# Selected heads projected behind the first branch, selection one round a step, retention's values ahead of the second branch

## Chip, cores and metric

The kernel runs on one core of a Trainium2 chip. The metric is device time in microseconds, the median of the runs shown. PE is the matrix engine (PEld its weight loads), DVE the vector engine, ACT the scalar engine, POOL GpSimd, SP the queue that issues the loads.

## The reference, cut to what matters

The program is one block of a first architecture (S5 and gating branches, cross attention, a gated feed-forward) followed by two layers of a second one; sequence 512, width 1024, fp32. The change is in the mixing stage of the second architecture, which each of its two layers runs once:

```python
h = rmsnorm(x, attn_norm[l]);  z = h @ w_in[l]
(qA, kA, vA, fA, qB, kB, vB, qI, kI, wI, qC, kC, vC, gC, qD, kD, vD, gates) = split(z)
yA = forgetting_attention(qA, kA, vA, fA, forget_bias[l])            # 8 heads, causal
yB = dsa_attention(rope(qB), rope(kB), vB, rope(qI), rope(kI), wI)   # 8 heads, top 128 keys of a row
r  = retention(rope(qC), rope(kC) * 64**-0.5, vC)
yC = head_groupnorm(r, ret_norm[l]) * silu(gC)
yD = sliding_window_gqa(rope(qD), rope(kD), vD, attn_sinks[l])       # window 128
branch = einsum('bsnc,ncd->bsnd', stack([yA, yB, yC, yD]), w_branch[l])
merged = sum(sigmoid(gates) * branch, axis=branches)
x = x + merged @ w_out[l]
```

In `dsa_attention` each query keeps the `topk = min(256, 512 // 4) = 128` keys with the highest index score, a sum over four index heads; the others are masked out.

## The kernel before

**Projections.** Everything is kept transposed: features on the 128 partitions, the 512 tokens along the free dimension. fp32 values are split into two fp32r parts, and each product is three matmuls (`mm3`, L184). One projection of 128 features (`gemm_b`, L190) is 8 slices of the width times 3, thus 24 matmuls of 512 columns; a natural-layout projection of 512 features (`gemm_a`, L198, through `natural`, L1249) is 96 such matmuls into four PSUM banks at once. `weights` (L177) loads 512 KB into one of two `raw` buffers on SP's queue; ACT copies the upper part `hi` (L166) and DVE subtracts to get `lo` (L111), each in one of three buffers.

**Buffers.** 48 tiles of the tag `g`, 12 of `h`, 10 of `tmp`; PSUM banks are 4 `mm` for projections, 3 `sc` for scores and transposes, 1 `pv` for attention's output.

**Order of the work.** Attention, selection and retention are Python generators that stand in two lists. `pump(n)` (L140) takes one step of the list `bg2`, which holds the selection alone, and `n` steps of the list `bg`, oldest generator first; `drain` (L150) runs the named generators to their end. So a program order comes about in which a step of attention or selection stands behind a projection. The framework's scheduler then lays out each engine's queue at build time on a simulated timeline: instructions that are ready can be taken ahead of earlier ones that are not, as far as buffers allow.

**Stages of `mix2` (L1319).** The first rotated projections give the index heads and the selected heads' key; `select` (L1115) is started; a misc projection and the fox values (`natural`, L1338 on) follow. Then the fox loop projects key and query of four pairs of heads, builds a `fox_pair` (L1072) for each and appends it to `bg`, with `rate` 4. The selected heads' loop projects four pairs of rotated queries (at the first of them the selection is drained, since the masks are needed) and appends a `rope_pair` for each. `branch` 0 follows with a lead of 4 gates, then the window heads with `rate` 2, `branch` 1, retention's values, gates, keys and queries, `branch` 3, `branch` 2 and the output projection.

**A branch (L1255).** For each of 8 slices of the output it needs a gate (a projection, times the row norm, tanh; 24 matmuls) and a product of the branch's output with its weights (12 matmuls). `lead` gates come first, then the attention that feeds the branch is drained, then slices and remaining gates alternate. The first branch writes its gates in the merged tiles, later ones in `tmp`. Each gate and each slice pumps once.

**Attention (`attend`, L966).** A pair of heads takes 14 steps: per chunk of 128 queries the scores and their maximum (PE, DVE, L982), then exponentials (ACT), sums and normalization (DVE, L994 and L996), then transposes (PE, L1007) and copies (ACT, L1010); at the end all value matmuls (PE, L1021) and a split of the result.

**Selection (`select`).** Three scoring steps, one for each chunk of queries from the second on. Then 16 rounds, each of which finds the 8 largest scores of a row (MAX8, L1144) and strikes them out (MATCH_REPLACE8 with its value load, L1145) in the three chunks; a step holds two rounds (L1146). A last step turns what was struck out into a mask (L1150).

**Retention (`retain`, L1153).** 31 steps over four chunks; it reads the values `vc` from tiles of the tag `h`, which the fox values `va` use before.

Of the kernel before, what the change touches and what calls it, by code (L numbers as in the profile page):

```python
# [11 lines left out]
AF = mybir.ActivationFunctionType  # L12
# [5 lines left out]
P = 128  # L18
# [10 lines left out]
MAGIC = 12582912.0  # L29
LEAD = (4, 3, 3, 3)  # L30
NSLOT = 48
# [40 lines left out]
class Builder:  # L72
# [1042 lines left out]
    def select(self, si, hh, ll, msc):  # L1115
# [24 lines left out]
        for r in range(16):  # L1140
            for c in range(1, CHUNKS):
                sc = self.masks[c]
                m8 = self.t(ap, [P, 8], "m8", bufs=3)
                nc.vector.max(m8, sc)  # L1144
                nc.vector.match_replace(sc, m8, sc, -3.0e38)  # L1145
            if r % 2:  # L1146
                yield
        for c in range(1, CHUNKS):
# [105 lines left out]

    def branch(self, l, n, y, x, first, gens=(), lead=3):  # L1255


        nc = self.nc
        gs = []

        def gate(d):
            bk = self.bank("mm")
            self.gemm_b(bk, self.weights(self.I["w_gates"][l, n, d], KT * P), x)
            g = self.merged[d] if first else self.tmp()
            self.mul(g, bk, self.rb)
            self.act(g, g, AF.Tanh, scale=0.5)
            gs.append(g)
            self.pump(self.rate)

        for d in range(lead):  # L1270
            gate(d)
        self.drain(*gens)
        wb = None
        for d in range(KT):
            if d + lead < KT:
                gate(d + lead)
            if d % 2 == 0:
# [41 lines left out]
    def mix2(self, l):  # L1319
# [29 lines left out]
        ya, yb, yc, yd = {}, {}, {}, {}  # L1349
        ga, gb, gd = [], [], []  # L1350
        for j in range(4):
            bk = self.project(I["w_fox"][l, 4 + j], x)
            self.pump(self.rate)
            bq = self.project(I["w_fox"][l, j], x)
            ga.append(self.fox_pair(ya, j, bq, bk, va))
            self.bg.append(ga[-1])
            self.pump(self.rate)

        for j in range(4):
# [8 lines left out]
            self.pump(self.rate)  # L1368
        self.branch(l, 0, ya, x, True, ga, LEAD[0])
        self.rate = 2  # L1370
# [4 lines left out]
        for j in range(4):  # L1375
# [10 lines left out]
            self.pump(self.rate)  # L1386
        self.branch(l, 1, yb, x, False, gb, LEAD[1])

        vc = [self.g2() for _ in range(CHUNKS)]
        self.natural(I["w_vc"][l], x, vc, 512)  # L1390
        sg = [self.g() for _ in range(CHUNKS)]
        rn = self.g()
# [222 lines left out]
```

## Time and profile before

| | us |
|---|---|
| median of 3 runs | 3055.34 |
| lowest, highest | 3055.07, 3061.35 |
| profiled execution, its own time | 3054.14 |
| its span in the trace | 3052.3 |
| PE busy in the span | 2979.2 |
| DVE busy | 1993.9 |
| ACT busy | 1354.3 |

Times in the views are microseconds from the span's start. The mixing stage of the first layer lies at about 940 to 1600 us, that of the second at about 1980 to 2640 us. A wait is put down to what ended it. The busy time of a window counts overlapping instructions of an engine once; the busy time of a group adds their records, which overlap a little. The granted clock is TensorE's, as a share of full speed.

### The profile page before, as it was taken

The numbers are of one execution on the slowest core, as the hardware profiler recorded it, in microseconds if no ns is written. First come the engines' busy times: TensorE is split into PE (matmuls) and PEld (weight loads), VectorE is DVE, ScalarE is ACT, GpSimd is POOL, SyncE is SP. The second block draws the span as 40 slices with busy tenths as digits, with TensorE's granted clock in tenths as the row PEclk, the third lists the DMA queues.
The fourth block names the chain that finished last, engine by engine and source line by source line (L and its number), as shares of the span: only waits on it lengthen the run. The fifth ranks groups of instructions, "written<-read, shape, count | busy, mean of one in ns | idle before, by whom it ended". The sixth has DMA issues, their size and how long they took to land.

```text
span 3052.3 us, 38841 instructions
## 1 busy us (share of the span) xinstructions
PE 2979.2 (98%) x14882; PEld 2481.1 (81%) x14882; DVE 1993.9 (65%) x3850; ACT 1354.3 (44%) x2271; POOL 112.2 (4%) x148
## 2 busy tenths in 40 slices
PE   9999899999999998999999999999899999999998
PEld 7888888888888877887888888888687788888887
DVE  7887564545447796556667566569866466675575
ACT  5523443422226565546234333356665453343343
POOL 0000000011010000000000010000000000000010
PEclk9999999999999999999999999999999999999999
DMA  5233442333333221222133333342122222323332
GB/s 171 83 92 99 113 162 84 100 92 95 104 90 122 88 75 42 69 83 91 63 117 105 97 92 103 92 136 78 54 70 67 82 80 82 125 92 99 97 95 82
DMA packets 98362, 287.09 MB, mean 94 GB/s; under 512 B 12144, under 2 KB 20592, under 8 KB 98176
## 3 DMA queue, kind: packets, MB, share of 16 engines
q1 hardware_dynamic: 95712, 283.04, 29.7%
q10 hardware_dynamic: 2464, 1.57, 0.3%
q8 instruction: 117, 1.92, 0.3%
q14 instruction: 69, 0.57, 0.1%
HBM read 274.64 MB, written 9.93 MB: 93 GB/s over the span
## 4 chain that ended last, share of the span: by engine, by line
PE 91%; DVE 5%; ACT 2%; DMA 1%; issue 1%; SPq 0%; DVEq 0%; ACTq 0%
PE psmm L186 27%; PE psmm L187 27%; PE psmm L188 27%; PE pspv L1021 2%; PE pssc L1007 1%; DVE g L111 1%; DVE lo L111 1%; PE pssc L1110 1%; PE pssc L1111 0%; DVE tmp L111 0%; DVE prob L982 0%; PE pspv L806 0%; DMA raw<-w_down 0%; PE pssc L774 0%; PE pssc L716 0%
## 5 line engine op out<-in xcount | busy, mean ns | idle before, releaser
L186 PE MATMUL psmm<-g,hi 128*128 128x512 f32 (+1 forms) x3456 | 1342.8, 391 | 14.7 <-DVE h L111 4.9
L188 PE MATMUL psmm<-g,lo 128*128 128x512 f32 (+1 forms) x3456 | 1344.4, 390 | 3.5 <-DVE lo L111 3.5
L187 PE MATMUL psmm<-g,hi 128*128 128x512 f32 (+1 forms) x3456 | 1343.3, 389 | 0.0
L166 ACT CAST hi<-raw 128x1024 fp32r<-128x1024 f32 (+3 forms) x507 | 508.7, 1004 | 1168.9 <-PE psmm L187 839.2
L186 PEld LDWEIGHTS psmm<-g,hi 128*128 128x128 f32 x3456 | 650.0, 188 | 151.6 <-DVE g L111 4.0
L188 PEld LDWEIGHTS psmm<-g,lo 128*128 128x128 f32 x3456 | 650.7, 188 | 138.1 <-DVE lo L111 5.9
L187 PEld LDWEIGHTS psmm<-g,hi 128*128 128x128 f32 x3456 | 650.9, 188 | 128.8 <-issue 0.8
L111 DVE TENSOR_TENSOR lo<-raw,hi 128x1024 fp32r<-128x1024 f32 (+3 forms) x507 | 608.7, 1201 | 209.7 <-ACT hi L166 208.6
L111 DVE TENSOR_TENSOR tmp<-psmm,g 128x512 f32<-128x512 f32 x236 | 161.6, 688 | 287.5 <-PE psmm L188 276.3
L1461 DVE SCALAR_TENSOR_TENSOR g<-psmm,g 128x512 f32<-128x512 f32 x88 | 60.8, 691 | 150.2 <-PE psmm L188 150.2
L186 PE MATMUL psmm<-hi,g 128*128 128x512 f32 (+1 forms) x384 | 143.7, 381 | 9.9 <-ACT g L123 7.1
L187 PE MATMUL psmm<-lo,g 128*128 128x512 f32 (+1 forms) x384 | 145.4, 379 | 0.0
L111 POOL TENSOR_TENSOR tmp<-tmp,tmp 128x512 f32<-128x512 f32 x66 | 89.0, 1349 | 1531.4 <-DVE tmp L1435 521.0
L188 PE MATMUL psmm<-hi,g 128*128 128x512 f32 (+1 forms) x384 | 142.9, 375 | 0.0
L1435 DVE SCALAR_TENSOR_TENSOR tmp<-tmp,vec,tmp 128x510 f32<-128x510 f32 (+1 forms) x176 | 132.8, 757 | 2.5 <-ACT tmp L123 1.2
L111 DVE TENSOR_TENSOR g<-tmp,g 64x512 fp32r<-64x512 f32 (+2 forms) x166 | 113.4, 684 | 17.9 <-ACT g L166 11.0
L123 ACT ACTIVATE prob<-prob,nmx 128x128 f32<-128x128 f32 (+2 forms) x192 | 102.6, 535 | 41.8 <-DVE nmx L982 37.6
L1010 ACT COPY probT<-pssc 128x128 f32<-128x128 f32 (+2 forms) x192 | 70.1, 400 | 74.1 <-PE pssc L1007 73.4
L939 ACT COPY tmp<-psmm 32x512 f32<-32x512 f32 x160 | 92.5, 578 | 2.4
L123 ACT ACTIVATE tmp<-tmp 128x512 f32<-128x512 f32 (+1 forms) x138 | 84.2, 613 | 20.9 <-DVE tmp L111 18.3
L1007 PE MATMUL pssc<-idn,prob 128*128 128x128 f32 x432 | 70.4, 283 | 23.3 <-DVE prob L996 22.3
L186 PEld LDWEIGHTS psmm<-hi,g 128*128 128x128 f32 x384 | 73.7, 192 | 22.3 <-ACT g L123 7.1
(275 smaller groups left out, 2688.2 us busy)
## 6 DMA issues: line engine op xcount, KB each, us to landing
raw<-w_up SPq DMA_DIRECT2D x110, 512.0 KB, 3.5
raw<-w_gates SPq DMA_DIRECT2D x64, 512.0 KB, 3.5
raw<-w_down SPq DMA_DIRECT2D x72, 384.0 KB, 3.1
raw<-w_rope SPq DMA_DIRECT2D x40, 512.0 KB, 3.6
raw<-w_branch SPq DMA_DIRECT2D x32, 512.0 KB, 3.5
raw<-w_out SPq DMA_DIRECT2D x24, 512.0 KB, 3.5
raw<-w_gate SPq DMA_DIRECT2D x22, 512.0 KB, 3.6
raw<-w_fox SPq DMA_DIRECT2D x16, 512.0 KB, 3.5
```

Source lines behind the costliest of these rows:

```text
L111: (eng or self.nc.vector).tensor_tensor(out, a, b, op)
L123: self.nc.scalar.activation(out, in_, func, **k)
L166: nc.scalar.copy(hi, src)
L186: mm(out, sh, mh, start=start, stop=False)
L187: mm(out, sh, ml, start=False, stop=False)
L188: mm(out, sl, mh, start=False, stop=stop)
L939: nc.scalar.copy(xs[k * 32:k * 32 + 32], bk[(k ^ 1) * 32:(k ^ 1) * 32 + 32])
L1007: nc.tensor.transpose(tr[:, j * P:(j + 1) * P], pt[i][:, j * P:(j + 1) * P], self.ident)
L1010: nc.scalar.copy(ptT, tr[:, :n * P])
L1021: nc.tensor.matmul(pv[i * 64:(i + 1) * 64, pc * P:(pc + 1) * P], value(i, b), tt[i][:, j * P:(j + 1) * P], start=j == 0, stop=j == len(bl) ...
L1435: nc.vector.scalar_tensor_tensor(o[:, sh:], u[:, :S - sh], w, o[:, sh:], ALU.mult, ALU.add)
L1461: self.nc.vector.scalar_tensor_tensor(self.x[d], ps, 0.5, self.x[d], ALU.mult, ALU.add)
```

## The change

Four edits in `mix2`, `branch` and `select`. The gate of a branch becomes a method, `gate`, and `branch` takes gates that are already there. In the fox loop one gate of the first branch is projected behind each pair, and behind the loop `branch` 0 is called with the four gates and a lead of 8, so its other four gates come before the drain of fox attention. The selected heads' loop stands behind that branch, still with `rate` 4, and still with the drain of the selection at its first projection. The selection yields after each round instead of each second one. Retention's values are projected before `branch` 1 instead of after it. The leads of the other branches are unchanged at 3.

```diff
--- before.py
+++ after.py
@@ -27,7 +27,7 @@
 NL = 2
 CHUNKS = 4
 MAGIC = 12582912.0
-LEAD = (4, 3, 3, 3)
+LEAD = {1: 3, 2: 3, 3: 3}
 NSLOT = 48
 NSLOT2 = 12
 NTMP = 10
@@ -1143,8 +1143,7 @@
                 m8 = self.t(ap, [P, 8], "m8", bufs=3)
                 nc.vector.max(m8, sc)
                 nc.vector.match_replace(sc, m8, sc, -3.0e38)
-            if r % 2:
-                yield
+            yield
         for c in range(1, CHUNKS):
             sc = self.masks[c]
             nc.vector.tensor_scalar(sc, sc, -1e37, NEG, ALU.is_gt, ALU.mult)
@@ -1252,28 +1251,28 @@
         for c in range(CHUNKS):
             self.act(out[c][:, :ncol], banks[c][:, :ncol], AF.Copy, scale=self.rc[:, c:c + 1])
 
-    def branch(self, l, n, y, x, first, gens=(), lead=3):
+    def gate(self, l, n, d, x, first):
+
+        bk = self.bank("mm")
+        self.gemm_b(bk, self.weights(self.I["w_gates"][l, n, d], KT * P), x)
+        g = self.merged[d] if first else self.tmp()
+        self.mul(g, bk, self.rb)
+        self.act(g, g, AF.Tanh, scale=0.5)
+        self.pump(self.rate)
+        return g
+
+    def branch(self, l, n, y, x, first, gens=(), lead=0, gs=()):
 
 
         nc = self.nc
-        gs = []
-
-        def gate(d):
-            bk = self.bank("mm")
-            self.gemm_b(bk, self.weights(self.I["w_gates"][l, n, d], KT * P), x)
-            g = self.merged[d] if first else self.tmp()
-            self.mul(g, bk, self.rb)
-            self.act(g, g, AF.Tanh, scale=0.5)
-            gs.append(g)
-            self.pump(self.rate)
-
-        for d in range(lead):
-            gate(d)
+        gs = list(gs)
+        while len(gs) < lead:
+            gs.append(self.gate(l, n, len(gs), x, first))
         self.drain(*gens)
         wb = None
         for d in range(KT):
-            if d + lead < KT:
-                gate(d + lead)
+            if len(gs) < KT:
+                gs.append(self.gate(l, n, len(gs), x, first))
             if d % 2 == 0:
                 wb = self.weights(self.I["w_branch"][l, n, d // 2], 1024)
             bb = self.bank("mm")
@@ -1347,7 +1346,7 @@
         self.natural(I["w_va"][l], x, va, 512)
         self.fox_rows(f)
         ya, yb, yc, yd = {}, {}, {}, {}
-        ga, gb, gd = [], [], []
+        ga, gb, gd, g0 = [], [], [], []
         for j in range(4):
             bk = self.project(I["w_fox"][l, 4 + j], x)
             self.pump(self.rate)
@@ -1355,6 +1354,8 @@
             ga.append(self.fox_pair(ya, j, bq, bk, va))
             self.bg.append(ga[-1])
             self.pump(self.rate)
+            g0.append(self.gate(l, 0, len(g0), x, True))
+        self.branch(l, 0, ya, x, True, ga, KT, g0)
 
         for j in range(4):
             o = proj(4 + j)
@@ -1366,7 +1367,6 @@
                                      lambda c: list(range(c + 1))))
             self.bg.append(gb[-1])
             self.pump(self.rate)
-        self.branch(l, 0, ya, x, True, ga, LEAD[0])
         self.rate = 2
 
         kd, kdl = self.stack_k(proj(1))
@@ -1384,10 +1384,10 @@
                 lambda j: self.vec(f"sink{l}")[:, 2 * j:2 * j + 2]))
             self.bg.append(gd[-1])
             self.pump(self.rate)
-        self.branch(l, 1, yb, x, False, gb, LEAD[1])
 
         vc = [self.g2() for _ in range(CHUNKS)]
         self.natural(I["w_vc"][l], x, vc, 512)
+        self.branch(l, 1, yb, x, False, gb, LEAD[1])
         sg = [self.g() for _ in range(CHUNKS)]
         rn = self.g()
         nc.sync.dma_start(rn, I["ret_norm"][l].partition_broadcast(P))
```

## Rows read from the trace of the kernel before

**Rows 1.** The page: busy time, share of the span and instructions of each engine.

```profile
PE 2979.2 (98%) x14882; PEld 2481.1 (81%) x14882; DVE 1993.9 (65%) x3850; ACT 1354.3 (44%) x2271; POOL 112.2 (4%) x148
```

**Rows 2.** Waits of PE, first layer (930:1560): total us, times, longest.

```profile
PE pssc L1007 <- DVE prob L996: 11.8, 5, 4.2
```

**Rows 3.** Waits of PE, second layer (1990:2680), same columns.

```profile
PE pssc L1007 <- DVE prob L996: 10.5, 5, 3.2
```

**Rows 4.** Windows: length, busy us of PE, PEld, DVE, ACT, POOL; clock; DMA.

```profile
1040.00:1060.00 20.00, 20.00 (x94) 16.65 (x93) 19.74 (x46) 16.01 (x29) 0.52 (x1) 1.00 0.24 79
...
1160.00:1180.00 20.00, 16.49 (x99) 13.97 (x100) 8.72 (x33) 9.38 (x27) 0.00 (x0) 0.76 0.00 1
...
1280.00:1300.00 20.00, 18.97 (x119) 15.30 (x115) 15.07 (x38) 14.24 (x33) 0.00 (x0) 1.00 0.09 27
1300.00:1320.00 20.00, 18.12 (x115) 14.77 (x116) 16.92 (x44) 11.77 (x30) 0.00 (x0) 1.00 0.24 80
...
1600.00:1620.00 20.00, 20.00 (x90) 16.55 (x89) 11.95 (x15) 8.67 (x12) 0.00 (x0) 1.00 0.54 181
```

**Rows 5.** Windows of whole stretches, same columns.

```profile
1032.00:1182.00 150.00, 135.84 (x704) 111.00 (x706) 133.99 (x343) 100.70 (x205) 2.08 (x4) 0.95 0.19 60
2075.00:2220.00 145.00, 131.82 (x693) 107.81 (x692) 131.08 (x334) 99.37 (x198) 2.08 (x4) 0.96 0.20 64
...
1147.00:1182.00 35.00, 26.13 (x154) 21.00 (x152) 20.56 (x65) 21.67 (x58) 0.00 (x0) 0.84 0.03 11
1183.00:1305.00 122.00, 120.38 (x716) 100.17 (x712) 73.29 (x172) 70.49 (x152) 0.00 (x0) 1.00 0.22 70
...
1100.00:1182.00 82.00, 68.25 (x381) 54.84 (x379) 66.39 (x187) 53.77 (x121) 0.52 (x1) 0.91 0.12 39
2140.00:2222.00 82.00, 68.70 (x408) 55.19 (x408) 68.64 (x195) 54.03 (x122) 0.52 (x1) 0.94 0.14 45
```

**Rows 6.** DVE's groups in 1032:1182: shapes xcount; busy us, mean ns; idle before.

```profile
L1145 DVE MATCH_REPLACE8 g<-m,g 128x384 f32<-128x384 f32 (+2 forms) x47 | 25.3, 543 | 0.1
L1144 DVE MAX8 m<-g 128x8 f32<-128x384 f32 (+2 forms) x47 | 24.4, 548 | 0.0
L111 DVE TENSOR_TENSOR lo<-raw,hi 128x1024 fp32r<-128x1024 f32 x17 | 20.6, 1211 | 0.0
L111 DVE TENSOR_TENSOR g<-tmp,g 64x512 fp32r<-64x512 f32 x24 | 16.4, 683 | 0.6
...
L111 DVE TENSOR_TENSOR tmp<-psmm,g 128x512 f32<-128x512 f32 x12 | 7.9, 678 | 0.0
...
L1145 DVE MATCH_VALUE_LOAD g<-m,g 128x8 f32 x47 | 3.7, 78 | 0.1
...
L111 DVE TENSOR_TENSOR tmp<-tmp,g 128x512 f32<-128x512 f32 x4 | 2.7, 678 | 0.0
L111 DVE TENSOR_TENSOR tmp<-tmp,tmp 128x512 f32<-128x512 f32 x4 | 2.7, 676 | 0.0
```

**Rows 7.** PE's groups in 1032:1182, same columns; one of three alike.

```profile
L186 PE MATMUL psmm<-g,hi 128*128 128x512 f32 x140 | 54.9, 399 | 3.6 <-ACT hi L166 1.8 <-DVE h L111 1.8
```

**Rows 8.** Timeline of DVE, end of the selection: start us, us, instruction.

```profile
1142.09 0.54 DVE L1150 TENSOR_SCALAR g<-g 128x256 f32<-128x256 f32 x2
...
1142.62 0.68 DVE L1145 MATCH_REPLACE8 g<-m,g 128x512 f32<-128x512 f32 x1
...
1143.81 0.41 DVE L1150 TENSOR_SCALAR g<-g 128x512 f32<-128x512 f32 x1
```

**Rows 9.** Timeline of PE: value matmuls of three fox pairs.

```profile
1145.18 2.40 PE L1021 MATMUL pspv<-probT,h 128*64 128x128 f32 x38
...
1164.76 3.53 PE L1021 MATMUL pspv<-probT,h 128*64 128x128 f32 x38
...
1181.63 3.62 PE L1021 MATMUL pspv<-probT,h 128*64 128x128 f32 x38
```

**Rows 10.** Timeline of SyncE's queue: loads around 1145 us.

```profile
1145.38 53.99 SPq L174 DMA_DIRECT2D raw<-w_rope  x4
```

## Prediction

> **What bounds the kernel now.** I read the page's busy table first: PE is busy 98% of the span (3052.3 us in the table), DVE 65% [rows 1]. So there is little to win outside PE's gaps, and the next question is where they lie. The waits of PE name one consumer in both layers of the second block: transposes of attention probabilities (L1007) that wait for DVE's normalization, 11.8 us in five waits in the first layer and 10.5 us in the second [rows 2, 3]. The windows then show the shape in time [rows 4]. At 1040 to 1060 us DVE has 19.74 of 20 us busy and PE is full. At 1160 to 1180 us DVE is down to 8.72 us, PE to 16.49, and the granted clock to 0.76 of full speed. Two regimes follow each other: one in which DVE is full, one in which a chain hops between PE, DVE and ACT and PE has nothing else.
>
> DVE's groups say what fills the first [rows 6]: 47 MAX8 and 47 MATCH_REPLACE8 of the selection with their value loads, 53.4 us by their records, the largest item by far. The selection's last replacement starts at 1142.62 us and its last mask at 1143.81 [rows 8]. From there forgetting attention's pairs run unhindered: their value matmuls come at 1145.18, 1164.76 and, for the fourth pair, 1181.63 us, so a pair takes some 17 to 20 us [rows 9]; two of four pairs were still to do. PE can't fill the time because SyncE's row shows four loads of projection weights spread over 54 us from 1145.38 [rows 10]: behind the branch weights the loads stand still until attention is through.
>
> **The change part by part.** No instruction is added or removed: the same 64 gate projections, 32 selection rounds, loads and evacuations, on the same engines. What changes is their order, so the sum is one of waits.
>
> *What the pumps do.* A pump runs one step of the selection and `rate` steps of attention. Before, the value projection pumps once and the fox loop 8 times: 3 scoring steps and 6 double steps, thus 12 of 16 rounds, with 28 of 56 attention steps. The first selected head then drains the other 4 rounds and the masks, ahead of the second half of attention. After, the fox loop pumps 12 times and the four other gates 4 times: 17 selection steps are 3 of scoring and 14 rounds (13 by the pump that writes attention's 56th step), the rest goes into the branch's own 8 pumps. So the selection is spread evenly instead of leading, and 3 rounds and the masks fall behind the first attention.
>
> *DVE up to the end of fox attention.* Between 1032 and 1182 us DVE has 133.99 us busy [rows 5]. Records overlap, so I scale each record total by 0.89 (133.99 over the 150 us that the groups of this stretch add up to, of which eight are shown). The selected heads' projections go behind: 12 tensor operations of 0.68 us in their rotation, 8 residues of 0.683 and 4 weight splits of 1.211 [rows 6], 18.5 us of records, 16.4 scaled. The 3 late rounds are 9 times (0.543 + 0.548 + 0.078) us, 10.5, and 0.95 for the masks [rows 8], 10.2 scaled. DVE needs then 107.4 us if these stay behind and 117.6 if the scheduler pulls the always ready rounds forward. It would end at 1139 or 1150 us; I take the middle, 1145, and some 3 us for the last hop: 1148.
>
> *PE up to there.* PE was busy 135.84 us in this stretch, at a mean clock of 0.95 [rows 5]. The moved projections are 96 of the 420 matmuls of 512 columns (three groups of 140 [rows 7]), at 90 in 20 us [rows 4] 21.3 us. That leaves 114.5 us, or 107 if the clock's 5% (7.5 us) came back whole: 1139 to 1147, say 1143. PE's and DVE's demand now meet. PE's idle time there falls from 14.2 us (150 less 135.84) to about 5 us, and the clock's share from 7.5 to about 3: 13.7 us in the first layer. In the second the same stretch is 145 us long with 131.82 busy at 0.96 [rows 5], 13.2 and 5.8 us against the same 5 and 3: 11.0 us. Together 24.7 us. The bounds are 40.7 us (all of both layers) and nothing below the rival's loss.
>
> Over 1100 to 1182 and 2140 to 2222 us PE sits idle 13.75 and 13.30 us of 82, while weight loads cover 54.84 and 55.19 us; in the dense stretch 1183 to 1305 they cover 100.17 of 122 [rows 5]. The Trainium skill (Perfetto Trace Analysis, "Identifying the Most-Contended Engine") says that matmul busy time flatters PE and that weight-load busy time is the better measure; by it I estimate 15.2 and 14.8 us lost, 3 us more than PE's own gaps, and a gain larger by that.
>
> *Selected heads and the second branch.* Their projections now come when masks are nearly done, so their attention can start once the first is rotated, about where it started before. What covers it grows: beside the window heads' five projections and the branch's gates, as now, three of its own four projections and the values of retention (96 matmuls, 21.3 us). But its steps run at 4 a pump for only 4 pumps, then at 2 for the window heads' 4, the values' 1 and the 3 leading gates: 32 of 56. The other 24 are drained in one go, where before none were. At 17 us per 14 steps that is 29 us, beside gates 3 to 7, 120 matmuls or 26.7 us, and attention's own matmuls. The branch lost 1.03 and 1.88 us at 1280 to 1320 [rows 4]; I let that grow by 2.5 us a layer, between a gain of 2.9 (cover complete) and a loss of 12 (no gate is pulled forward, at the loss of 1147 to 1182: 8.9 us idle of 35 and 16% of the clock, 5.6 us [rows 5]). Cost: 5 us.
>
> *Small things.* The four loads of retention's values move ahead of the branch's on SyncE, behind the window heads'; nothing on PE waits for them earlier than now. GpSimd's queue keeps its order. Their four output tiles take the buffers of the fox values, last read by the value matmuls that start at 1181.63 us [rows 9], before the window heads are even projected. The values take all four PSUM banks at once, behind a rotation instead of behind the branch; the latter wait moves to the gates of retention. The window heads end later, by 3 pumps, and so does retention, whose 31st step now falls on the last pump ahead of its branch; gate 3's 24 matmuls, 5.3 us, lie behind it. I cost these at nothing, between minus 2 and plus 4 us a layer if that one gate is too short.
>
> **Sum.** 24.7 less 5 is 19.7 us off the profiled execution's 3054.14 us (span 3052.3 and 1.8 around it): 3034.4. The median shown, 3055.34, lies 1.2 us above that execution, so 3035.
>
> **Rivals.**
> - *The cover was needed more than the selection hurt (slower).* Four projections leave the stretch in which PE starves, and the first three branch weights hold the three weight buffers as soon as the gates are through. 13 of 16 rounds still precede attention's last step. If the fourth pair runs alone once DVE is free, at 17 us, it ends near 1163; PE, ready at 1143, idles 20 us, and loses 7.5 to the clock as now: 27.5 against 21.7, 5.8 us a layer worse, with the drain 2 times 8.3: 3072. It decides from an end of attention after some 1155 (11.7 us idle). For it: two pairs do run alone now. Against: they do so because the selection was drained ahead of them, which the change undoes.
> - *Moved, not removed (no change).* The drain of 24 steps costs its 12 us a layer and eats the gain: 24.7 less 24, 3055. For it: before, such a stretch was where the clock fell. Against: gates were pulled ahead of the stalled first branch, and five are at hand.
> - *The order hardly changes.* The scheduler takes selection rounds whenever DVE is free, so their place in the program matters little: DVE ends at 1150, attention at 1153, PE idles 10 us and the clock costs 5: 6.7 and 4.0 us won, less 5, 3050. For it: DVE had no gap in which a round was not ready. Against: it follows the program's order where an attention step is ready too.
> - *All of it comes back.* PE's idle time and the clock both vanish and the values cover the second branch: 40.7 plus 5.8, 3009.
>
> The Trainium skill (Perfetto Trace Analysis, "Optimization Strategy") says that where the most-contended engine changes over time, interleaving the regimes can help, and that repeated bubbles can mean too few buffers. The first speaks for the forecast, the second for the slower rival: here the trace shows both, DVE full and then loads standing still.
>
> **How the numbers follow.** The forecast, 3022 to 3048, has 0.50; all of it 0.14; the small gain 0.10; no change 0.08; slower 0.18. What this kernel's measurement can tell from no change is 0.2%, 6 us. Faster: 0.50, 0.14 and half of the small gain, 0.69; same: the other half and no change, 0.13; slower 0.18. Of the slower rival 0.13 lie above 3066, of the largest gain 0.07 below 3010; these are the range's ends.
>
> **What would show it.** Right: the selection's last replacement comes after fox attention's third value matmuls; PE's idle time in the stretch falls under 8 us and the clock stays above 0.97; L1007's waits for the normalization fall by half; the first selected head's scores come after the branch. Wrong: a stretch with PE under 17 of 20 us before the first branch's matmuls, or a new one ahead of the second branch's, with the clock down; then the rivals hold.

## The result and the profile after

The change made the kernel slower: 3077.92 us against 3056.54 in the same runs, a ratio of 1.0064 with a 95% interval of 1.0052 to 1.0076. The forecast was 3035 with a range up to 3066. The profiled execution of after took 3081.67 us, the longest of its four, that of before 3054.14, shorter than all of its four; so I read the traces for places and shares, and the sizes from the ratios.

**Where the time is.** The changed stage from the load of the misc weights to the load of the output weights, one window for each layer (length, busy us of PE, PEld, DVE, ACT, POOL with counts, clock, DMA share, GB/s). Before:

```profile
947.63:1576.13 628.50, 605.61 (x3232) 501.81 (x3231) 429.45 (x1025) 331.24 (x660) 6.22 (x13) 0.98 0.25 79
1996.50:2616.50 620.00, 601.06 (x3229) 498.56 (x3228) 422.06 (x1006) 330.24 (x658) 6.22 (x13) 0.99 0.25 78
```

After:

```profile
951.54:1591.66 640.12, 614.97 (x3232) 508.30 (x3231) 429.80 (x1025) 331.96 (x660) 6.23 (x13) 0.96 0.25 78
2012.03:2643.27 631.24, 610.76 (x3229) 506.10 (x3228) 421.76 (x1006) 329.75 (x658) 6.24 (x13) 0.97 0.24 77
```

The stages are 11.6 and 11.2 us longer, 22.9 of the 27.6 us between the two spans (3.9 more lie ahead of the first stage, where nothing was changed). PE runs the same 3232 and 3229 matmuls, but is busy with them 9.4 and 9.7 us longer; its idle time grows by only 2.3 and 1.5 us. So most of the loss is not a longer wait: the same matmuls ran slower, and the granted clock went from 0.98 and 0.99 to 0.96 and 0.97. The clock accounts for nearly all of that. In the two stages of before, PE is busy for 19.7 and 12.9 us at the lower of its two levels (0.50), in those of after for 37.0 and 29.1 us; half of the difference, 8.7 and 8.1 us, is what the lower level took from it. It is not one execution alone: over the whole span the clock was 0.983 to 0.985 in the four executions of after, and 0.989 to 0.992 in the twelve of before beside experiments 7 to 10.

**Where in the stage.** Windows of after, same columns; they answer to [rows 4, 5]:

```profile
1040.00:1060.00 20.00, 20.00 (x94) 16.65 (x93) 18.23 (x41) 18.69 (x33) 0.52 (x1) 1.00 0.19 57
1100.00:1120.00 20.00, 16.95 (x102) 12.97 (x100) 19.80 (x53) 12.62 (x25) 0.00 (x0) 0.90 0.16 52
1120.00:1140.00 20.00, 13.95 (x79) 10.72 (x78) 18.75 (x65) 8.99 (x22) 0.51 (x1) 0.58 0.10 27
1140.00:1160.00 20.00, 14.76 (x86) 10.96 (x85) 9.74 (x33) 14.41 (x39) 0.00 (x0) 0.74 0.01 1
1160.00:1180.00 20.00, 16.54 (x97) 13.52 (x96) 8.81 (x24) 8.72 (x22) 0.00 (x0) 0.83 0.00 1
...
1320.00:1340.00 20.00, 17.40 (x114) 13.93 (x112) 9.30 (x29) 9.51 (x27) 0.00 (x0) 0.95 0.11 37
...
1100.00:1180.00 80.00, 62.20 (x358) 48.17 (x357) 57.10 (x172) 44.75 (x104) 0.51 (x1) 0.77 0.07 20
2160.00:2240.00 80.00, 63.99 (x345) 51.05 (x344) 54.25 (x152) 41.67 (x97) 0.51 (x1) 0.83 0.11 34
```

The two regimes of before are still there, and DVE's full one now reaches into the starved one: at 1120 to 1140 us DVE has 18.75 of 20 us busy while PE is down to 13.95 at 0.58 of its clock, a mixture of its two levels. A full DVE beside a starved PE was there in before too, at the full clock:

```profile
1140.00:1160.00 20.00, 14.30 (x102) 11.08 (x100) 17.25 (x47) 14.48 (x35) 0.00 (x0) 1.00 0.09 27
```

Over 80 us PE sits idle 17.8 and 16.0 us; before it was 13.75 and 13.30 of 82 at clocks of 0.91 and 0.94 [rows 5], now 0.77 and 0.83. PE's waits for the normalization, first and then second layer, answer to [rows 2, 3]:

```profile
PE pssc L1007 <- DVE prob L996: 13.9, 8, 4.0
...
PE pssc L1007 <- DVE prob L996: 15.0, 6, 4.8
```

The end of the selection on DVE (answers to [rows 8]; the mask's line is now L1149), and PE's value matmuls of the fox pairs (answer to [rows 9]), from the timelines:

```profile
1135.40 0.68 DVE L1145 MATCH_REPLACE8 g<-m,g 128x512 f32<-128x512 f32 x1
...
1136.12 0.43 DVE L1149 TENSOR_SCALAR g<-g 128x512 f32<-128x512 f32 x1
```

```profile
1100.91 2.40 PE L1021 MATMUL pspv<-probT,h 128*64 128x128 f32 x40
...
1134.09 3.62 PE L1021 MATMUL pspv<-probT,h 128*64 128x128 f32 x38
...
1155.08 3.38 PE L1021 MATMUL pspv<-probT,h 128*64 128x128 f32 x38
...
1169.82 4.92 PE L1021 MATMUL pspv<-probT,h 128*64 128x128 f32 x40
```

The selection still ends some 34 us ahead of attention's last value matmuls, with two pairs left to run alone, exactly what the change should have undone. These last value matmuls end at 1174.7 us. SyncE's queue shows what PE had left (answers to [rows 10]):

```profile
1088.25 26.35 SPq L174 DMA_DIRECT2D raw<-w_branch  x4
1119.22 95.46 SPq L174 DMA_DIRECT2D raw<-w_rope  x9
```

From 1119 us on the buffers hold weights of the branch, which waits for attention; only the first of the nine loads is issued there, the second at 1180.75, 61.5 us later; in before that gap is 46.8 us (1145.38 to 1192.17). At the second branch PE is idle about as long as before: 2.6 us at 1320 to 1340, 2.9 before [rows 4]. But the clock there falls. The 100 us around it, first and then second layer, in before and in after:

```profile
1267.63:1367.63 100.00, 97.10 (x545) 79.73 (x544) 59.96 (x153) 51.72 (x120) 0.00 (x0) 1.00 0.24 74
2316.50:2416.50 100.00, 97.08 (x564) 79.71 (x564) 60.31 (x153) 51.11 (x121) 0.00 (x0) 1.00 0.24 75
```

```profile
1271.54:1371.54 100.00, 97.40 (x544) 80.20 (x544) 53.23 (x134) 44.71 (x107) 0.00 (x0) 0.97 0.21 68
2332.03:2432.03 100.00, 97.50 (x560) 80.47 (x559) 54.80 (x150) 43.52 (x109) 0.00 (x0) 0.97 0.22 70
```

At 0.97 for 100 us that is some 3 us a layer, about 6 of the 22.9.

### The profile page after: what moved, and what is told of

It is laid out like the page before. It is cut to its first block, busy times and chain, and to the rows that moved or that the text cites. A ratio compares the mean times of both kernels' runs of the same rounds, so it can differ in the third digit from the quotient of the medians.

```text
span 3079.9 us, 38860 instructions
## 1 busy us (share of the span) xinstructions
PE 3001.5 (97%) x14882; PEld 2497.5 (81%) x14882; DVE 1994.2 (65%) x3850; ACT 1354.3 (44%) x2271; POOL 112.3 (4%) x148
## 4 chain that ended last, share of the span: by engine, by line
PE 91%; DVE 5%; ACT 2%; DMA 1%; issue 1%; SPq 0%; DVEq 0%; ACTq 0%
PE psmm L186 27%; PE psmm L187 27%; PE psmm L188 27%; PE pspv L1021 2%; PE pssc L1007 1%; DVE g L1145 1%; DVE m L1144 1%; DVE lo L111 1%; PE pssc L1110 1%; PE pssc L1111 1%; DVE g L111 1%; DVE tmp L111 1%; DMA b<-zd 0%; PE pssc L1171 0%; DMA raw<-w_down 0%
## 5 line engine op out<-in xcount | busy, mean ns | idle before, releaser
L186 PE MATMUL psmm<-hi,g 128*128 128x512 f32 (+1 forms) x384 | 143.0, 380 | 10.6 <-ACT g L123 7.8
L1007 PE MATMUL pssc<-idn,prob 128*128 128x128 f32 x432 | 79.8, 303 | 31.5 <-DVE prob L996 28.9
L1007 PEld LDWEIGHTS pssc<-idn,prob 128*128 128x128 f32 x432 | 59.5, 155 | 51.7 <-DVE prob L996 23.6
```

Source lines behind the costliest of these rows:

```text
L186: mm(out, sh, mh, start=start, stop=False)
L1007: nc.tensor.transpose(tr[:, j * P:(j + 1) * P], pt[i][:, j * P:(j + 1) * P], self.ident)
```

## The experiments

Ratios are to the kernel before in the same runs, with their 95% intervals. "M" in what follows is the load of the first layer's misc weights; it lies at 948 to 952 us in all kernels, so absolute times of the first layer can be compared within some 4 us. "M2" is the same load in the second layer (1996.50 us in before, 2012.03 in after).

**1 and 2. The two small parts alone**, on the kernel before.

```diff
-            if r % 2:
-                yield
+            yield
```

> The kernel before with one edit: the selection yields after each round. Theory C (cover: the order of the projections costs, because PE runs out of projections while forgetting attention still waits for DVE): within 5 us of before, selection's last replacement a little later, PE idle in the first starved stretch unchanged at 12 to 16 us. Theory S (the finer selection step is what costs, because its rounds mix worse with attention): 10 to 20 us slower. Theory V (the values ahead of the second branch cost): within 3 us.

```diff
-        self.branch(l, 1, yb, x, False, gb, LEAD[1])
-
         vc = [self.g2() for _ in range(CHUNKS)]
         self.natural(I["w_vc"][l], x, vc, 512)
+        self.branch(l, 1, yb, x, False, gb, LEAD[1])
```

> The kernel before with one edit: retention's values are projected ahead of the second branch. Theory C and S: within 4 us of before; the second branch's waits (2.9 us a layer) shrink or move. Theory V: 10 to 20 us slower, with a new idle stretch of PE around the second branch.

0.9996 (0.9987 to 1.0005) and 0.9988 (0.9979 to 0.9996). Neither costs anything.

**3. The order alone**: the kernel after with two rounds a step and retention's values behind the second branch, the two edits above undone.

> The changed kernel with two of its three parts undone: two rounds a step, values behind the second branch; only the order of gates, first branch and selected heads is changed. Theory C: 15 to 25 us slower than before, the whole change, PE idle 16 to 19 us between the last gate and the end of forgetting attention and the granted clock under 0.85 there. Theory S or V: within 6 us of before.

1.0051 (1.0038 to 1.0063), 3076.42 us: the loss is in the order of gates, first branch and selected heads.

**4. The cover back**: the kernel after with the first branch behind the selected heads' projections again; its gates stay spread over the fox loop, all eight ahead of the drain.

```diff
-        self.branch(l, 0, ya, x, True, ga, KT, g0)
...
             self.bg.append(gb[-1])
             self.pump(self.rate)
+        self.branch(l, 0, ya, x, True, ga, KT, g0)
```

> The changed kernel with one edit: the first branch stands behind the selected heads' projections again, so gates come with the fox pairs, one round a step and values first stay, and four more projections lie ahead of the branch weights. Theory C: the loss is gone, and as 16 instead of 12 projections now lie ahead of the stalled branch weights, 0 to 15 us faster than before; PE idle in the first stretch under 12 us. Theory S: still 10 to 20 us slower than before. Theory V: still 10 or more slower.

1.0036 (1.0022 to 1.005), 3072.22 us. A miss for the plain count of cover: with all the projections of before ahead of the drain, more than half of the loss stayed.

**Without the selection's load on DVE** (two more kernels, not numbered): before and after with two rounds in place of 16. They leave out 14 rounds a layer, so too few keys are selected.

```diff
-        for r in range(16):
+        for r in range(2):
```

> The kernel before with 2 selection rounds instead of 16 (14 rounds of MAX8 and MATCH_REPLACE8 a layer are left out, so the selected set is wrong in size). Theory D (the selection's hold on DVE delays forgetting attention, which starves PE): 15 to 40 us faster than before, PE idle in the first stretch under 5 us a layer, clock 1.00 there. Rival H (attention's own hops between PE, DVE and ACT set its end, the selection only fills DVE's gaps): within 8 us of before, the stretch as idle as now.

> The changed kernel with 2 selection rounds instead of 16, the same work left out as in the kernel with 2 rounds in the order before. Theory D: the change's loss vanishes with the rounds: within 6 us of that kernel, either way. Rival H: still 15 to 25 us slower than that kernel, since four projections fewer lie beside attention.

0.9901 (0.9886 to 0.9917) and 0.9971 (0.996 to 0.9982): 3030.63 and 3051.05 us, still 20.4 apart, where the full kernels differ by 21.4. So the loss doesn't need the selection's rounds, although the 14 rounds cost some 30 us in before and 28 in after, by the ratios. The first layer's stage in both; first before without the rounds, then after without them:

```profile
949.53:1561.55 612.02, 596.39 (x3232) 495.28 (x3231) 391.41 (x899) 330.18 (x660) 6.31 (x13) 1.00 0.25 82
```

```profile
950.48:1574.44 623.96, 606.05 (x3232) 503.70 (x3231) 390.20 (x899) 331.13 (x660) 6.21 (x13) 0.98 0.24 80
```

Again 9.7 us more busy time for the same matmuls, and 2.3 us more idle time.

**5. Separating the two**: the kernel after with the selection started only behind the fox loop and drained behind all four selected projections.

```diff
-        self.bg2.append(sel)
...
+        self.bg2.append(sel)
         self.branch(l, 0, ya, x, True, ga, KT, g0)
+        qb = []
+        for j in range(4):
+            qb.append(self.stack_q(proj(4 + j)))
+            self.pump(self.rate)
+        self.drain(sel)
         for j in range(4):
-            o = proj(4 + j)
-            if j == 0:
-                self.drain(sel)
-            gb.append(self.rope_pair(yb, j, self.stack_q(o), hh[0], ll[0],
+            gb.append(self.rope_pair(yb, j, qb[j], hh[0], ll[0],
```

> The changed kernel with the selection started behind the fox loop instead of ahead of the fox values, and the four selected heads' projections all ahead of its drain: forgetting attention no longer has rounds ahead of it in the program, and branch and projections lie beside the rounds. Theory D: 10 to 35 us faster than before, forgetting attention's last value matmuls at 110 to 130 us after the misc load instead of 185 to 238. Rival H: forgetting attention ends no sooner than in the changed kernel. Rival M (masks late): attention of the selected heads starts late and PE starves ahead of the second branch: within 10 us of before or slower.

0.9963 (0.995 to 0.9975), 3049.36 us: faster than both kernels. The two stages, as above:

```profile
951.29:1572.87 621.58, 603.75 (x3232) 499.06 (x3231) 429.97 (x1025) 331.06 (x660) 6.16 (x13) 0.99 0.25 80
1993.24:2610.24 617.00, 601.78 (x3229) 497.59 (x3228) 422.42 (x1006) 328.95 (x658) 7.09 (x13) 0.99 0.24 78
```

Against after both parts shrink: busy time by 11.2 and 9.0 us, idle time by 7.3 and 5.3. Attention now runs ahead of the selection instead of beside it, its last value matmul in the first layer ends at M + 198.9 us against M + 223.2 in after, and the selection then loads DVE while PE has projections. The expectation had it end at 110 to 130 us, so the chain of attention takes most of its time with no round ahead of it.

**6. Filling the gaps**: the kernel after with three 512-column matmuls, whose results nobody reads, in each bank ahead of the transposes of the third and fourth fox pair; 48 more matmuls a layer.

```diff
+                    if fill is not None:
+                        for _ in range(3):
+                            nc.tensor.matmul(tr, fill[0], fill[1], start=True, stop=True)
```

> The changed kernel with idle work added: three matmuls of 512 columns into each transpose bank of forgetting attention's third and fourth pair, overwritten by the transposes, 48 a layer, 10.9 us at the full clock. Theory K (most of the change's loss is the granted clock of the starved stretch, not idle time): the granted clock between 1100 and 1180 us rises from a mean of 0.76 to over 0.9 and the total stays within 5 us of the changed kernel or falls below it, in spite of 22 us more matmuls. Rival I (idle time is the loss, the clock only follows): 8 to 20 us slower than the changed kernel.

1.0042 (1.003 to 1.0055), 3073.41 us, against 1.0064 (1.0052 to 1.0076) for after: no slower and by the medians 4.5 us faster, with 96 matmuls more. The same two stretches as in the two windows of 80 us of after:

```profile
1100.00:1180.00 80.00, 68.19 (x395) 53.67 (x392) 57.83 (x167) 45.14 (x105) 0.51 (x1) 0.87 0.10 30
2160.00:2240.00 80.00, 70.33 (x405) 56.44 (x404) 52.54 (x144) 39.82 (x90) 0.51 (x1) 0.94 0.13 40
```

The clock went from 0.77 and 0.83 to 0.87 and 0.94. The first is below the 0.9 that was expected. That supports the reading of the clock as the larger part of the loss; the intervals just touch, so the gain itself isn't certain.

**7 to 10. Gates 4 to 7 held back**: a lead of 4 in place of 8, so these four gates stand in the branch's own loop between its weight loads. On after, on experiment 4, on experiment 5, and on experiment 5 with the branch behind the four selected projections.

```diff
-        self.branch(l, 0, ya, x, True, ga, KT, g0)
+        self.branch(l, 0, ya, x, True, ga, 4, g0)
```

> The kernel after, but only gates 0 to 3 of the first branch run inside the forgetting-attention loop; gates 4 to 7 (96 matmuls of 512 columns, 21.3 us) stand in the branch's own loop, between its weight loads, as in the kernel before. Theory L (wide projections must still be at hand once attention runs alone; with all eight gates ahead of the branch none are): the four gates move into the starved stretch, PE's windows of 13.95 and 14.76 us with a clock of 0.58 and 0.74 fill up, and about half of the loss comes back: 3066 us, ratio to before 1.000 to 1.005. Rival M (the gates are pulled forward whenever their weights are in, so their place in the program does nothing): 3078 us, ratio 1.005 to 1.008, clock in 1120 to 1160 us still under 0.75.

> The fourth experiment's kernel (first branch behind the selected heads' projections again), with gates 4 to 7 in the branch's own loop. It then differs from the kernel before only by gates 0 to 3 spread over the attention loop, one round a step, and retention's values ahead of the second branch, of which the last two were worth nothing alone. Theory L: the fourth experiment's loss goes, 3056 us, ratio 0.998 to 1.002; gates' weights are then loaded between the branch's, up to 170 us behind the misc load. Rival M: 3072 us as in the fourth experiment, ratio 1.002 to 1.006.

> The fifth experiment's kernel (selection behind the forgetting-attention loop, drained behind all four selected projections; 3049 us), with gates 4 to 7 in the branch's own loop. Its starved stretch costs 7 us of PE idle and 2 us of clock in 1120 to 1160 us. Theory L: four gates come to lie there and most of it goes, 6 us a layer: 3037 us, ratio 0.992 to 0.996. Rival M: 3049 us, ratio 0.996 to 0.999.

> The same as the ninth, with the first branch behind the selected heads' four projections, as in the kernel before, and the selection drained behind the branch. Theory L: the cover of forgetting attention is the largest of all kernels here (four projections, four gates), so its stretch has PE at 19 of 20 us and the clock at 1.00; but the selection now ends later, at the branch's end, and selected attention starts some 20 us later, with less time to the second branch: 3035 to 3050 us, ratio 0.993 to 0.998, the second branch's windows (before: 1.0 and 1.9 us idle) up to 8 us idle a layer. Rival M: as the fifth, ratio 0.996 to 0.999, with the stretch as there.

1.003 (1.0019 to 1.0041), 1.0043 (1.003 to 1.0055), 0.9965 (0.9952 to 0.9978) and 0.9963 (0.9951 to 0.9975). Holding gates back gains 10 us on after, as theory L had it, and nothing on the other three, as its rival had it (the ratio of the tenth fits both). Experiment 8 differs from before only in gates 0 to 3 inside the fox loop and in the two small parts, and loses all the same; so something about gates in the loop costs.

**11 and 12. One part of the order alone**, on the kernel before: the line of the first branch moved ahead of the selected heads' loop, and the lead of 8.

```diff
+        self.branch(l, 0, ya, x, True, ga, LEAD[0])
         for j in range(4):
             o = proj(4 + j)
...
-        self.branch(l, 0, ya, x, True, ga, LEAD[0])
```

> The kernel before with one line moved: the first branch, with its four leading gates as they are, stands ahead of the selected heads' projections. Theory P (the cover is what counts: the selected heads' four projections, 96 matmuls of 512 columns or 21.3 us a layer, no longer stand ahead of attention's drain): attention runs alone for longer at a lower clock, as in the kernel after; 3066 to 3078 us, ratio 1.003 to 1.007, clock and idle together 35 us or more in the first layer's stage (before: 28.7). Theory G (the gates' place carries the loss: gates run inside the attention loop, ahead of the stretch that needs them): the branch's place costs nothing, 3053 to 3061 us, ratio 0.998 to 1.002.

```diff
-LEAD = (4, 3, 3, 3)
+LEAD = (8, 3, 3, 3)
```

> The kernel before with one number changed: all eight gates of the first branch stand ahead of its drain (LEAD 8 where it was 4), none in its loop; nothing is spread over the attention loop. Theory G's narrow form (gates held back behind the branch weights are the cover of the starved stretch): as in the fourth experiment, 3066 to 3076 us, ratio 1.003 to 1.006, clock share of the first layer's stage 15 us or more (before: 8.6). Theory P: the same projections stand ahead of the drain as before, plus four gates more, so nothing is lost: 3053 to 3061 us, ratio 0.998 to 1.002.

0.9987 (0.9978 to 0.9996) and 1.0004 (0.9994 to 1.0014). The headline of the change, the selected heads behind the first branch, costs nothing, and neither do eight gates ahead of the drain. The first is against the plain cover theory (P) a second time, the second against theory G's narrow form, and both leave the gates inside the loop.

**13 to 15. Gates or their pumps?** A gate in the loop also pumps. In 13, on experiment 7, the gates stay in the loop and their four pumps go behind it; in 14, on before, the gates stay behind and the four pumps go into the loop; 15 is the edit of 13 on after.

```diff
-    def gate(self, l, n, d, x, first):
+    def gate(self, l, n, d, x, first, pump=True):
...
-        self.pump(self.rate)
+        if pump:
+            self.pump(self.rate)
...
-            g0.append(self.gate(l, 0, len(g0), x, True))
+            g0.append(self.gate(l, 0, len(g0), x, True, False))
+        for _ in range(4):
+            self.pump(self.rate)
```

> The seventh experiment's kernel (branch first, gates 0 to 3 inside the attention loop, 4 to 7 in the branch's loop; 3068 us), but the four gates inside the loop don't pump; their four pumps stand behind the loop. Theory S (it is the pumps that hurt: 12 attention steps more are written ahead of the fourth pair's preparation, so that its casts come behind the second pair's values, at 176 to 181 us from the misc load against 159 to 162 with the gates behind the loop): the casts come back to about 160 us, the loss goes, 3056 to 3061 us, ratio 0.998 to 1.001. Theory T (it is the gates' own place, which takes 96 wide matmuls ahead of their time and the fourth pair's projections 20 us later): casts at 176 or later, 3066 to 3070 us, ratio 1.002 to 1.004.

```diff
             self.bg.append(ga[-1])
             self.pump(self.rate)
+            self.pump(self.rate)
...
             gs.append(g)
-            self.pump(self.rate)
+            if not first or d >= lead:
+                self.pump(self.rate)
```

> The kernel before with four pumps more inside the attention loop, one for each pair, and none at the branch's four leading gates; every matmul group keeps its place in the program. Theory S: the fourth pair's casts slip behind the second pair's values (about 200 us from the misc load against 168 to 180), and the loss of the eighth experiment comes without any gate in the loop: 3066 to 3074 us, ratio 1.002 to 1.005. Theory T: nothing, 3055 to 3061 us, ratio 0.998 to 1.001.

> The kernel after with that one edit: the four gates inside the loop don't pump, the four pumps stand behind it. All eight gates are still ahead of the branch's drain. Theory S: what is left is the price of eight gates ahead of the drain with no selected projections behind them, which the seventh experiment put at 0.0034: 3064 to 3070 us, ratio 1.001 to 1.004 (after: 1.0064). Theory T: as the kernel after, 3074 to 3080 us, ratio 1.005 to 1.007.

1.0013 (1.0004 to 1.0022), 1.0056 (1.0044 to 1.0069) and 1.0038 (1.0024 to 1.0052). The first fell between its two expectations, the second above both, the third where theory S had it. In the middle one every projection and load keeps its place in the program, only attention and selection steps are written earlier, and 0.56% are lost: the place of the pumps alone can cost nearly as much as the change did. The casts that prepare a pair of heads move with them (ACT, `nc.scalar.copy(k[i][r], tk[r])` in `fox_pair`; count, ns, first and last start in the first layer). Before, after, 11, 14 and 15, in this order:

```profile
L1086 ACT CAST g<-tmp x8: 608/617/621, 1032.9 to 1125.7; 64x512 fp32r<-64x512 f32 x8
```

```profile
L1086 ACT CAST g<-tmp x8: 610/618/622, 1039.2 to 1143.1; 64x512 fp32r<-64x512 f32 x8
```

```profile
L1086 ACT CAST g<-tmp x8: 608/617/622, 1033.9 to 1109.5; 64x512 fp32r<-64x512 f32 x8
```

```profile
L1086 ACT CAST g<-tmp x8: 608/617/621, 1035.3 to 1151.5; 64x512 fp32r<-64x512 f32 x8
```

```profile
L1086 ACT CAST g<-tmp x8: 612/617/621, 1037.2 to 1121.4; 64x512 fp32r<-64x512 f32 x8
```

The last cast, of the fourth pair, moves from 1125.7 in before to 1151.5 with four pumps more in the loop, and from 1143.1 in after to 1121.4 with them behind it. Where pumps are in the loop it comes behind the second pair's value matmuls (1134.09 in after), in the stretch where attention runs alone; where they are not, ahead of them.

But the trace of 14 does not put its loss there. Its attention stretch in the first layer (M + 100 to 250), in before and in 14, then the 100 us around the second branch in 14:

```profile
1047.63:1197.63 150.00, 136.17 (x728) 111.59 (x727) 130.10 (x345) 93.05 (x197) 1.56 (x3) 0.94 0.19 62
```

```profile
1050.04:1200.04 150.00, 136.51 (x728) 111.57 (x727) 129.01 (x343) 92.00 (x195) 1.56 (x3) 0.93 0.19 62
1270.04:1370.04 100.00, 95.60 (x521) 78.10 (x520) 59.50 (x150) 49.80 (x118) 0.00 (x0) 0.97 0.21 69
```

The stretch is as it was, and attention ends at M + 236.8 us against 237.6. What 14 loses in this layer it loses behind attention, at the second branch: 1.5 us more idle time, and 0.97 where the clock was 1.00. In the second layer attention does end later, at M2 + 233.3 against 227.4. So the late casts alone do not account for the loss of 14.

**Where attention ends.** In five kernels with the first branch ahead of the selected heads, 11, 13, 15, 7 and after, the end of attention carries the whole difference. The fourth pair's value matmuls of the first layer in 11, 13, 15 and 7, in this order:

```profile
1157.35 3.91 PE L1021 MATMUL pspv<-probT,h 128*64 128x128 f32 x40
```

```profile
1161.58 4.06 PE L1021 MATMUL pspv<-probT,h 128*64 128x128 f32 x40
```

```profile
1163.59 4.46 PE L1021 MATMUL pspv<-probT,h 128*64 128x128 f32 x40 [0.27 <-ACT probT L1010]
```

```profile
1162.71 4.17 PE L1021 MATMUL pspv<-probT,h 128*64 128x128 f32 x40 [0.27 <-ACT probT L1010]
```

They end at M + 211.0, 213.5, 216.8 and 217.2 us, in after at M + 223.2. From there to the load of the output weights all five need the same, 415.7, 415.6, 416.7, 417.0 and 416.9 us (in the second layer 415.3 to 417.2). Before needs 390.9 and 392.6, but its attention ends at M + 237.6. So the move put 25 to 26 us behind attention, mostly the 21.3 us of projections and a second branch at a lower clock, and it pays only where attention ends that much earlier: by 26.6 us in 11, by 14.4 in after.

**16. Late selection without gates in the loop**: experiment 9 with its four gates behind the loop.

```diff
-            g0.append(self.gate(l, 0, len(g0), x, True))
```

> The ninth experiment's kernel (selection behind the attention loop, branch first; 3048 us) with its four leading gates behind the loop, as in the eleventh. If the fourth pair's early preparation helps here as well, forgetting attention ends earlier than 190 us from the misc load and the time is 3036 to 3044 us, ratio 0.992 to 0.995; if not (without the selection in the loop, casts came at 156 to 161 us already), 3046 to 3050 us, ratio 0.996 to 0.998.

1.0034 (1.0021 to 1.0046), 3067.59 us, 20 us slower than experiment 9 and outside both expectations. The replacements of the selection in the first layer (count, ns, first and last start), in experiment 9 and here:

```profile
L1145 DVE MATCH_REPLACE8 g<-m,g x48: 402/544/680, 1154.0 to 1250.5; 128x256 f32<-128x256 f32 x16, 128x384 f32<-128x384 f32 x16, 128x512 f32<-128x512 f32 x16
```

```profile
L1145 DVE MATCH_REPLACE8 g<-m,g x48: 405/544/687, 1115.7 to 1210.3; 128x256 f32<-128x256 f32 x16, 128x384 f32<-128x384 f32 x16, 128x512 f32<-128x512 f32 x16
```

The pumps behind the loop now advance the selection too, so its rounds start 38 us earlier, while the third and fourth pair still run; these end at M + 190.7 and 212.8 instead of 176.7 and 190.5. What hurts in one order helps in the other. A likely reason is that with the selection out of the loop, pumps inside it only bring attention forward; but the gates moved with their pumps here, and no run took them apart.

## Why the prediction was wrong

**The step that failed** is "PE's and DVE's demand now meet", with the 24.7 us it gave: PE idle 5 us and the clock's share 3 in each stretch. Measured were 17.8 and 16.0 us idle in 80, and the clock there at 0.77 and 0.83, by the windows 18 and 14 us. I added up what each engine has to do and took the end of attention from the sums. But attention ended at 1174.7, far behind the 1148 of the sum and the 1155 from which the slower rival decides, and experiments 11, 13 and 15 show that the order in which gates and pumps are written moves that end. Against before it came 14.4 us earlier by M and 13.4 by M2 (214.0 against 227.4), while the change put 26.0 and 24.6 us more behind it: that is the 11.6 and 11.2 us by which the two stages grew.

**A part of its root is the paragraph on the pumps.** I counted that the fox loop pumps 12 times instead of 8, and read it as a selection spread evenly. The same pumps write attention: ahead of the fourth pair's preparation six pumps, 24 steps, stood before, and nine pumps, 36 steps, stand after. Pair two then ends ahead of it, and the preparation, 12 ACT casts of 0.6 us and their DVE residues a pair, falls into the chain's own stretch. Experiments 13 to 15 turn the same pumps on and off: 0.56% lost with them on before, where no projection moved in the program, and 0.17 and 0.26% won back without them on experiment 7 and on after (there the intervals just touch), with attention's end 3.7 and 6.4 us earlier. That the late preparation itself makes the loss, by its load on ACT and DVE or by a later first score, is a reading of the casts' times that the first layer of experiment 14 speaks against; pumps move selection steps as well, and no run moved the preparation alone. Nor are pumps the whole root: in experiment 11, with no gate and no pump more in the loop, attention still ended 10.6 us behind the sum's 1148 by M.

**The rest of the loss** is the slower rival's cover, in part: eight gates ahead of the drain cost nothing while the selected projections also stand there (1.0004), but with these behind, after loses 0.34% to experiment 7 and experiment 15 loses 0.25% to experiment 13, 8 to 10 us. So the cover counts where both its parts are gone; alone, neither part does. From experiment 11 to after the ratio thus climbs in three steps of about the same size: gates in the loop without their pumps (0.9987 to 1.0013), all eight gates ahead of the drain (to 1.0038), the four pumps in the loop (to 1.0064). The first step also brings in the two small parts, which cost nothing alone; it was not followed further.

**Point by point.** The selection was forecast to end after the third pair's values; it ended at 1135.40, just as the second pair's came (1134.09): that fits the third rival's reason, rounds taken ahead whenever DVE is free, but its price was wrong in sign. Waits for the normalization were to halve; they rose from 11.8 to 13.9 and from 10.5 to 15.0 us. The selected heads' scores did move behind the first branch (first at 1205.7, before 1179.3), and experiment 11, which has that too, lost nothing. The 5 us for the drain of the second branch were about right in size and wrong in kind: idle time did not grow (2.6 us against 2.9), but the clock fell to 0.97 over 100 us, some 3 us a layer. Costing the small parts at nothing was right (experiments 1 and 2). The slower rival, at 3072 and with 0.18, was nearest: its condition (attention past 1155), its place and most of its price held. Its 20 us of idle time were near the 17.8 and 16.0 measured, but it left the clock at 7.5, where the windows give 18 and 14.

**The rule on interleaving.** The trace shows the regime of a full DVE and the starved one overlap at 1120 to 1140 us in after, and the kernel that takes the selection out of the attention loop (experiment 5) gains 0.37%. The Trainium skill (Perfetto Trace Analysis, "Optimization Strategy") says that interleaving regimes can help where the most-contended engine changes over time; here separating them did. Both regimes want DVE, which may be the reason; it is not shown, and the loss of the change does not come from that overlap alone, since it stays with 14 of 16 rounds left out.

**What stays open**: by which step the pumps delay attention (the late preparation alone was not tried), what makes experiment 14 lose behind attention, and why gates without pumps in the loop still cost some 0.26%.

## What to carry to other kernels

Where background work is written by pumps, a projection that is moved carries its pump with it: count for each later instruction how many background steps now stand ahead of it. Work that is moved behind a wait pays only if the wait ends earlier by more than that work. A sum of engine times gives a bound, not an end, while a chain of small steps hops between engines; and what starved PE cost twice here, 2.3 and 1.5 us of gaps and 8.7 and 8.1 us of lower clock in the matmuls that did run. Try each part alone first: the part with the headline cost nothing here.

## What the runs showed of the hardware

That the clock takes more than the gaps: 3232 and 3229 identical matmuls took 9.4 and 9.7 us longer to run, while PE's idle time grew by 2.3 and 1.5 us. And that work nobody reads can be free: with 96 matmuls of 512 columns among the third and fourth pair's transposes the clock of the starved stretches was 0.87 and 0.94 in place of 0.77 and 0.83, and the kernel was no slower (1.0042 against 1.0064).
